# Expert weights in pages of 4 MB instead of 2 MB, and a 512-column output projection, in a two-block network on one core

## The chip, the core and the metric

The kernel runs on one core of a Trainium2 chip; the other cores are idle. The metric is the device time of one execution in microseconds (us), and the median of several executions is compared.

## What is computed

One token sequence of 256 tokens with 1024 features passes two blocks, all in float32. The first block mixes tokens (latent attention and banded attention of three dilations, gated and summed into `mix`), projects `mix` with `w_out`, adds the result to `x`, and then applies a mixture of 16 experts in which each expert chooses its tokens:

```
aff = softmax(h2 @ w_router); gate, idx = top_k(aff^T, 32)      # 32 tokens for each of 16 experts
xe  = h2[idx]                                                   # [16, 32, 1024]
hid = silu(xe @ w_gate) * (xe @ w_up)                           # w_gate, w_up: [16, 1024, 2048]
y   = (hid @ w_down) * gate                                     # w_down: [16, 2048, 1024]
x   = x + gt2 * scatter_add(y, idx); x = rmsnorm(x, g_final)
```

The second block (a state-space mixer, a linear recurrence and two convolved feed-forward layers, 1024 to 8192 to 1024) follows. Its code is the same in both kernels, except that its page buffers lie elsewhere.

## The kernel before

**Stages.** Everything is issued from one program, and the order within each engine's queue is made by a scheduler that goes by program order and readiness. All loads are issued from SyncE's queue (SP). The stages are, in the profiled execution: attention up to about 430 us, the output projection with `w_out` to 463 us, routing to 481 us, the 16 experts to 1387 us, the second block to the end.

**Weights by pages.** `page`/`wpage` (L200 to L211) loads 1 MB of weights into a buffer of 8 KB a partition; five such buffers make the pool `pages`. `split` (L216) makes a rounded half `wh` on ScalarE (L231) and the rest `wl` on VectorE (L232), and `three` (L237 to L245) multiplies hi by hi, hi by lo and lo by hi, so that one float32 product is three matmuls of a faster type. The value projections `v` (loop at L860) take pages of 256 columns: for each page and each of two token tiles, 8 chunks of the contraction times three matmuls of 256 columns go into one half of a PSUM bank (`proj_N`, L603). The output projection (loop at L936) does the same with four pages of `w_out`; after each page the product is scaled by `gt1` and added to `x1` (L947, L950), squares are summed (L951), the new columns are turned (L955) and multiplied by the router's weights (L961). After the fourth page come `inv_rms` (L967), written as an iteration on VectorE, the router's logits `lg` (L970), softmax, the turned affinities (L1016), four rounds of top-8 on VectorE (L1026 to L1036), and the choice as a one-hot matrix `oh` (`places`, L1042), by which `gather` (L1055) picks the tokens of experts 0 and 1 with 16 matmuls in 8 chunks `k`. Only when all eight chunks are done does expert 0 begin. The other 14 experts' tokens are gathered in expert 1's time, in rounds of four experts (L1083 to L1086).

**The experts.** An expert has 24 MB of weights: 8 pages of `w_gu` (a gate half and an up half, 8 KB a partition each) and 4 pages of `w_dn`, 2 MB each, of which a partition reads 16 KB in one piece. `load_epage` (L840) puts page after page into a ring of ten places, 20 MB in all: `swap`, four of `pages3`, two times two buffers of `pages` (these pages come as two transfers of 1 MB, 8 KB a partition, L852; all others as one, L854), two of `pages2`, one of `pages4`. `swap` can be loaded early; `pages2` lies where `split`'s halves were, `pages3` and `pages4` where the attention stage's tiles were. A transfer into a place is issued when the place's last readers are done. For a `w_gu` page PE does 8 products of 512 columns, four side by side in 32-column tiles of the array (L1093); each product is two matmul instructions in the trace. Then come `hid` (L1096, L1097), its transposes, 32 products of 512 columns for the four `w_dn` pages (L1114), the scaling by `gt2` (L1117), and four products with the scatter matrix `sel` onto the accumulators `acc` (L1120), which also hold `x`.

**The end of the experts.** Behind the last expert page SP issues `cols2` (L1142), two rows of norm weights (L1132, 0.5 MB each, one row read for all partitions), and two pages for the second block. From `acc` the norms (L1180 to L1193) give `xf`, which is turned (L1151) and multiplied with the two lead pages (L1160), for token tile 0 and then for tile 1.

## Time and profile before

| | before |
|---|---|
| median of 3 executions | 2277.21 us (2275.04 to 2279.51) |
| the profiled execution's own time | 2275.1 us |
| its span in the trace | 2273.3 us |
| TensorE busy (matmuls) | 1903.4 us, 84% of the span |
| VectorE, ScalarE, GpSimd busy | 44%, 35%, 11% |
| granted TensorE clock, mean | 0.92 of full speed |
| loads | 645.21 MB, of which the experts' weights are 402.65 MB |

The shares are averages over stages with different limits: in 40 slices of the span TensorE is busy over 90% in the first ten and in most of the last fifteen, and about 60% between them, where the sixteen DMA engines are busy all the time. So the stages are read one by one.

### The profile page before, as it was taken

What the parts mean: (1) busy time and instruction counts of PE and PEld (TensorE: products, weight loads), DVE (VectorE), ACT (ScalarE), POOL (GpSimd) and SP (SyncE); (2) the same over time, 40 slices, a digit from 0 to 9 for tenths busy, and PEclk for the clock granted to TensorE, in tenths of its full rate; (3) what the DMA queues carried; (4) which work ended last, traced back from release to release, by engine and by line L of the source; (5) the groups of instructions that cost most, each with busy time, mean ns of one, the idle gap of its engine ahead of it and who ended that gap; (6) DMA issues with size and microseconds to landing.
All of it is one profiled execution on the core that took longest, in us unless ns stands there. A gap on an engine that the chain in (4) does not pass through costs nothing.

```text
span 2273.3 us, 30086 instructions
## 1 busy us (share of the span) xinstructions
PE 1903.4 (84%) x12707; PEld 1317.6 (58%) x12707; DVE 1001.5 (44%) x1486; ACT 790.4 (35%) x1181; POOL 247.4 (11%) x176
## 2 busy tenths in 40 slices
PE   7999999988666666656656567999999999999998
PEld 5989999943111111111111115988888889888887
DVE  7867664331000000000000004867767777877775
ACT  2445454311000000000000004656666667666564
POOL 0100023100000000000000003110222222032222
PEclk9999999999767777887788879999999999999999
DMA  9357766679999999999999998543465646456552
GB/s 325 113 186 259 231 215 203 263 314 426 426 428 427 426 428 425 427 427 426 427 427 425 426 427 311 166 130 130 162 196 185 198 168 212 146 193 197 184 186 84
DMA packets 211166, 645.21 MB, mean 284 GB/s; under 512 B 8148, under 2 KB 162132, under 8 KB 178390
## 3 DMA queue, kind: packets, MB, share of 16 engines
q1 hardware_dynamic: 211032, 643.29, 74.5%
q8 instruction: 100, 1.64, 0.3%
q14 instruction: 34, 0.28, 0.0%
HBM read 641.95 MB, written 1.05 MB: 283 GB/s over the span
## 4 chain that ended last, share of the span: by engine, by line
PE 56%; DMA 38%; DVE 3%; ACT 2%; issue 1%; SPq 0%; DVEq 0%; ACTq 0%
DMA epage<-in_w_gu 25%; DMA epage<-in_w_dn 13%; PE up L1247 10%; PE up L1250 5%; PE ca L245 4%; PE ca L244 3%; PE ca L243 3%; PE lead L1160 2%; PE qk L243 2%; PE qk L245 2%; PE qk L244 2%; PE gu L1093 1%; PE v L245 1%; PE v L244 1%; PE v L243 1%; PE xbc L243 1%
## 5 line engine op out<-in xcount | busy, mean ns | idle before, releaser
L232 DVE TENSOR_TENSOR wl<-page,wh 128x2048 fp32r<-128x2048 f32 (+2 forms) x191 | 434.2, 2274 | 196.4 <-ACT wh L231 196.0
L1093 PE MATMUL gu<-epage,xeT 128*32 128x512 f32 x2048 | 318.9, 740 | 198.2 <-DMA epage<-in_w_gu 198.1
L231 ACT CAST wh<-page 128x2048 fp32r<-128x2048 f32 (+2 forms) x191 | 358.3, 1878 | 218.9 <-PE ca L245 64.8
L1247 PE MATMUL up<-hb,wh 128*128 128x512 f32 x960 | 331.9, 396 | 0.0
L1093 PEld LDWEIGHTS gu<-epage,xeT 128*32 128x32 f32 x2048 | 60.6, 122 | 435.6 <-DMA epage<-in_w_gu 327.7
L1096 ACT ACTIVATE hid<-gu 128x512 f32<-128x512 f32 x16 | 9.6, 598 | 785.1 <-PE gu L1093 785.1
L1114 PE MATMUL dn<-epage,hidT 128*32 128x512 f32 x1024 | 171.9, 803 | 99.3 <-DMA epage<-in_w_dn 90.5
L1250 PE MATMUL up<-hb,wl 128*128 128x256 f32 x960 | 248.0, 279 | 0.0
L1097 DVE TENSOR_TENSOR hid<-hid,gu 128x512 f32<-128x512 f32 x16 | 11.0, 689 | 491.3 <-PE gu L1093 491.3
L1247 PEld LDWEIGHTS up<-hb,wh 128*128 128x128 f32 x960 | 173.2, 188 | 33.6
L1250 PEld LDWEIGHTS up<-hb,wl 128*128 128x128 f32 x960 | 180.9, 188 | 10.6
L1114 PEld LDWEIGHTS dn<-epage,hidT 128*32 128x32 f32 x1024 | 32.2, 131 | 223.7 <-DMA epage<-in_w_dn 151.3
L1117 DVE TENSOR_TENSOR ye<-dn,gt 128x512 f32<-128x512 f32 x16 | 11.1, 692 | 286.0 <-PE dn L1114 286.0
L1280 DVE SCALAR_TENSOR_TENSOR cv<-ups,cols,cv 128x255 f32<-128x255 f32 x240 | 117.5, 502 | 28.1 <-ACT cv L1275 25.4
L243 PE MATMUL qk<-hh,wh 128*128 128x256 f32 x384 | 109.8, 286 | 0.0
L244 PE MATMUL qk<-hl,wh 128*128 128x256 f32 x384 | 109.0, 284 | 0.0
L245 PE MATMUL qk<-hh,wl 128*128 128x256 f32 x384 | 108.7, 283 | 0.0
L1308 POOL TENSOR_SCALAR lru_c<-cols 128x10 f32<-128x10 f32 x1 | 0.3, 251 | 954.1 <-PE dn L1114 954.1
L245 PE MATMUL ca<-wh,hdl 128*128 128x512 f32 x256 | 101.7, 397 | 0.0
L244 PE MATMUL ca<-wl,hdh 128*128 128x512 f32 x256 | 100.8, 394 | 0.0
L243 PE MATMUL ca<-wh,hdh 128*128 128x512 f32 x256 | 100.4, 392 | 0.0
L1275 ACT ACTIVATE cv<-ups,cols 128x256 f32<-128x256 f32 x120 | 71.1, 603 | 81.4 <-DVE ups L1255 81.2
(515 smaller groups left out, 3666.0 us busy)
## 6 DMA issues: line engine op xcount, KB each, us to landing
epage<-in_w_gu SPq DMA_DIRECT2D x102, 2048.0 KB, 29.8
epage<-in_w_dn SPq DMA_DIRECT2D x51, 2048.0 KB, 29.7
page<-in_ffn_w_up SPq DMA_DIRECT2D x64, 1024.0 KB, 5.5
epage<-in_w_gu SPq DMA_DIRECT2D x52, 1024.0 KB, 34.9
page<-in_w_in SPq DMA_DIRECT2D x46, 1024.0 KB, 5.4
page<-in_ffn_w_down SPq DMA_DIRECT2D x32, 1024.0 KB, 4.9
epage<-in_w_dn SPq DMA_DIRECT2D x26, 1024.0 KB, 34.3
page<-in_w_ada SPq DMA_DIRECT2D x24, 1024.0 KB, 6.5
```

Source lines behind the costliest of these rows:

```text
L231: act.copy(hi[p_], v[p_])
L232: (lo or dve).tensor_tensor(lw[p_], v[p_], hi[p_], ALU.subtract)
L243: pe.matmul(ps, lhsT=ah, rhs=bh, start=first and k == 0, stop=False)
L244: pe.matmul(ps, lhsT=ah, rhs=bl, start=False, stop=False)
L245: last_mm[0] = pe.matmul(ps, lhsT=al, rhs=bh, start=False, stop=last and k == n - 1)
L1093: pe.matmul(gu[i][32 * j:32 * j + 32, :], lhsT=xeT[:, k, 32 * e:32 * e + 32], rhs=pg[i][:, 512 * j:512 * j + 512], start=(k == 0), stop=(k ...
L1114: pe.matmul(pd[32 * q:32 * q + 32, :], lhsT=hT[:, 2 * c2 + cp, j, :], rhs=pg[c2][:, o:o + 512], start=(j == 0 and c2 == 0), stop=(j == 3 a ...
L1160: pe.matmul(pss[0][:, 256 * c + 128 * t:256 * c + 128 * t + 128], lhsT=pg[:, k, 128 * c:128 * c + 128], rhs=hf[:, k, nat(t)], start=(k == ...
L1247: wide = lambda: pe.matmul(ps, lhsT=wh[:, k, cc], rhs=hx[k][2], start=(k == 0), stop=(k == 7))
L1250: last_mm[0] = pe.matmul(ps[:, :256], lhsT=wl[:, k, cc], rhs=hx[k][0], start=False, stop=False)
L1275: act.activation(out=y[:, c], in_=ps[:, 256 * c:256 * c + 256], func=AF.Identity, scale=wcol(c, taps - 1), bias=bcol(c))
L1280: dve.scalar_tensor_tensor(y[:, c, o:], ps[:, 256 * c:256 * c + S - o], wcol(c, j), y[:, c, o:], ALU.mult, ALU.add)
```

## The change

- **Pages of 4 MB.** The host lays `w_gu` out so that two chunks `k` lie side by side, 32 KB a partition in one piece, 4 pages an expert, and `w_dn` so that a page holds two blocks of 256 output columns with all 16 chunks of the contraction, 2 pages an expert. `epage` uses a ring of five: four single places of 32 KB a partition and one made of `swap` and `place4`, whose page comes as two transfers of 2 MB. The first half of page 1 is loaded early, into `swap`. The last page of all comes as four transfers of 1 MB.
- **Places.** `swap` now lies below `pages`. The pool `pages` is closed before the experts and opened anew (`pagesb`) behind them. `place1` lies on the old `pages`, `place2` on `split`, `place3` to `place5` on the attention stage's tiles.
- **Down projection.** For each of four blocks of 256 columns, 16 products of 256 columns in four 32-column tiles, then the scaling and two scatter products of 256 columns. `gt2` holds 1024 columns, and `sel` and `sgate` lose their halves.
- **512 columns.** `v` and `w_out` pages hold 512 columns of half the contraction, so that a matmul has 512 columns and fills a bank. The attention loop has two steps of four heads. The first `w_out` page is multiplied ahead of the last four heads.
- **The end of the projection by token tiles.** Scaling, sum, squares, transposes and logits go by token tile (`wo_end`), the logits deferred (`flush`); the inverse norm is a square root on ScalarE and a reciprocal.
- **Routing.** The first top-8 round reads PSUM without a copy. Two of the eight chunks of experts 0 and 1 are gathered ahead of expert 0, the others between its chunks; `slots` comes behind its gate and up products. The other experts are gathered in seven rounds of two.
- **Norm rows.** They are loaded ahead of expert 12 into columns of `xeT` that are no longer read.

```diff
-    o["w_gu"] = gu.reshape(16, 8, 128, 4096)
-    o["w_dn"] = np.asarray(inp["w_down"])[0].reshape(16, 4, 4, 128, 1024).transpose(0, 1, 3, 2, 4).reshape(16, 4, 128, 4096)
+    o["w_gu"] = gu.reshape(16, 4, 2, 128, 4096).transpose(0, 1, 3, 2, 4).reshape(16, 4, 128, 8192)
+    o["w_dn"] = np.asarray(inp["w_down"])[0].reshape(16, 16, 128, 4, 256).transpose(0, 3, 2, 1, 4).reshape(16, 2, 2, 128, 4096).transpose(0, 1, 3, 2, 4).reshape(16, 2, 128, 8192)
...
-    pages = ctx.enter_context(tc.tile_pool(name="pages", bufs=1))
     sw = ctx.enter_context(ExitStack())
     swap = sw.enter_context(tc.tile_pool(name="swap", bufs=1))
+    pg_ = ctx.enter_context(ExitStack())
+    pages = pg_.enter_context(tc.tile_pool(name="pages", bufs=1))
...
-    ring = [(swap, "swap", 1)]
     expert_pages = []
     for e in range(NE):
-        expert_pages += [A["w_gu"][e, k] for k in range(8)] + [A["w_dn"][e, b] for b in range(4)]
...
-        pl, tag, nb = ring[cnt[0] % len(ring)]
+        expert_pages += [A["w_gu"][e, k] for k in range(4)] + [A["w_dn"][e, b] for b in range(2)]
+    cnt, ring, first_half = [0], [], []
+
+    def epart(t, src, o, n):
+        last_dma[0] = sync.dma_start(out=t, in_=src[:, o:o + n])
+        return [t[:, i:i + 2048] for i in range(0, t.shape[1], 2048)]
+
...
+    def epage():
+
+        pl = ring[cnt[0] % len(ring)]
         src = expert_pages[cnt[0]]
         cnt[0] += 1
...
-        if pl is pages:
-            v = [pl.tile([128, 2048], F32, name="epage", tag=tag, bufs=nb) for _ in range(2)]
-        else:
-            t = pl.tile([128, 4096], F32, name="epage", tag=tag, bufs=nb)
-            v = [t[:, :2048], t[:, 2048:]]
...
-        return ahead.pop(0) if ahead else load_epage()
...
-    for i in range(4):
-        if i == 3:
-            with tc.issue_after(last_dma[0].ins):
-                ahead.append(load_epage())
-            behind = last_dma[0]
+        if len(pl) == 2:
+            v = first_half.pop() if first_half else to_swap(src)
+            return v + epart(pl[1].tile([128, 4096], F32, name="epage", tag="half", bufs=1), src, 4096, 4096)
+        t = pl[0].tile([128, 8192], F32, name="epage", tag="place", bufs=1)
+        if cnt[0] < len(expert_pages):
+            return epart(t, src, 0, 8192)
+        return [epart(t[:, o:o + 2048], src, o, 2048)[0] for o in range(0, 8192, 2048)]
...
+    def proj_N2(w, c0, ps, tok):
+
+        for p_ in range(2):
+            wh, wl = split(wpage(w, c0, 512, 4 * p_, 4))
+            for t in range(2):
+                three(ps[t], [sl(k_, lambda a: a[:, tok(t)]) for k_ in h[4 * p_:4 * p_ + 4]],
+                      [(wh[:, k], wl[:, k]) for k in range(4)], p_ == 0, p_ == 1)
...
+    for ii in range(2):
...
-            pg = wpage(w_in, W_Q0 + 3072 * g + 2048 + 256 * i, 256)
-            ps = mm("v")
...
+            if ii == 1 and g == 2:
+                with tc.issue_after(last_dma[0].ins):
+                    first_half.append(to_swap(expert_pages[1]))
+            ps = [mm("v"), mm("v")]
+            proj_N2(w_in, W_Q0 + 3072 * g + 2048 + 512 * ii, ps, nat if g == 0 else par)
+            vt = dp.tile([128, 2, 512], F32, name=f"v{g}", tag=f"v{g}", bufs=1)
+            for t in range(2):
+                act.copy(vt[:, t], ps[t])
             v.append(vt)
...
-        pTs = []
-        for u in range(2):
-            hd = 2 * i + u
+        if ii == 1:
+
+            pso = [mm("wo"), mm("wo")]
+            w = wo_w(0, 0)
+            for t in range(2):
+                wo_mm(pso, w, 0, t)
...
+        pTs = [weights(0)]
+        for u in range(4):
+            if u < 3:
+                pTs.append(weights(u + 1))
...
-    for i in range(4):
-        pg = wpage(A["w_out"][0], 256 * i, 256)
-        wh, wl = split(pg)
-        ps = mm("wo")
-        for t in range(2):
-            three(ps[:, 256 * t:256 * t + 256], [sl(m_, lambda a: a[:, nat(t)]) for m_ in mx_],
-                  [(wh[:, k], wl[:, k]) for k in range(8)], True, True)
-        cs_ = slice(256 * i, 256 * i + 256)
...
-        dve.tensor_tensor(y, ps.rearrange("p (t n) -> p t n", t=2), gt1[:, None, cs_].to_broadcast([128, 2, 256]),
-                          ALU.mult)
-        for t in range(2):
-            dve.tensor_tensor(x1[:, t, cs_], x1[:, t, cs_], y[:, t], ALU.add)
-            sumsq(act, x1[:, t, cs_], y[:, t], x1q[t][:, i:i + 1])
...
+    def wo_end(g, t, ps):
...
+        for i in range(2):
+            o = 512 * g + 256 * i
+            cs_ = slice(o, o + 256)
+            y = rows3.tile([128, 256], F32, name="yo", tag="yo", bufs=3)
+            dve.tensor_tensor(y, ps[:, 256 * i:256 * i + 256], gt1[:, cs_], ALU.mult)
+            last = dve.tensor_tensor(x1[:, t, cs_], x1[:, t, cs_], y, ALU.add)
+            sumsq(act, x1[:, t, cs_], y, x1q[t][:, 2 * g + i:2 * g + i + 1])
             for c in range(2):
...
+        later.append(lambda: wo_logits(g, t, xT))
+        if g == 1:
...
+            dve.tensor_reduce(v, x1q[t], AX.X, ALU.add)
+            inv1[t] = inv_root(rows2, v, D)
+        return last
...
+    w = wo_w(0, 1)
+    for t in range(2):
+        wo_mm(pso, w, 1, t)
+        wo_end(0, t, pso[t])
+    pso = [mm("wo"), mm("wo")]
+    w = wo_w(2, 0)
+    for t in range(2):
+        wo_mm(pso, w, 0, t)
+    flush()
+    w = wo_w(2, 1)
+    for t in range(2):
+        wo_mm(pso, w, 1, t)
+        flush()
+        last = wo_end(1, t, pso[t])
+    flush()
...
-        dve.tensor_reduce(v[:, t:t + 1], x1q[t], AX.X, ALU.add)
-    inv1 = inv_rms(rows2, v, D)
...
-        dve.scalar_tensor_tensor(lg[:, t], pl_[t][:, :16], inv1[t], lsh, ALU.mult, ALU.add)
+        with tc.issue_after(last.ins):
+            dve.scalar_tensor_tensor(lg[:, t], pl_[t][:, :16], inv1[t], lsh, ALU.mult, ALU.add)
...
+    pg_.close()
...
-    pages2 = w2.enter_context(tc.tile_pool(name="pages2", bufs=2, reuse_waits="tile"))
-    pages3 = w2.enter_context(tc.tile_pool(name="pages3", bufs=4, reuse_waits="tile"))
-    pages4 = w2.enter_context(tc.tile_pool(name="pages4", bufs=1, reuse_waits="tile"))
-    ring = [(swap, "swap", 1)] + [(pages3, "page3", 4)] * 4 + [(pages, "page", NPAGE)] * 2 + \
-        [(pages2, "page2", 2)] * 2 + [(pages4, "page4", 1)]
+    place = [w2.enter_context(tc.tile_pool(name=f"place{i}", bufs=1, reuse_waits="tile")) for i in range(6)]
+    place[0].tile([128, 2048], F32, name="spare")
+    ring += [(place[5],), (swap, place[4]), (place[3],), (place[1],), (place[2],)]
...
+    residual([(0, 0)])
...
     with tc.issue_after(last.ins):
-        for t in range(2):
-            for n in range(2):
-                pe.matmul(acc[t][n], lhsT=ident, rhs=x1[:, t, 512 * n:512 * n + 512], start=True, stop=False)
+        residual([(0, 1), (1, 0), (1, 1)])
...
-    dve.tensor_copy(affT, pb_[:16, :256])
...
-        dve.max(out=g_, in_=affT)
-        dve.max_index(out=idx[:, 8 * r:8 * r + 8], in_max=g_, in_values=affT)
+        a_ = affT if r else pb_[:16, :256]
+        dve.max(out=g_, in_=a_)
+        dve.max_index(out=idx[:, 8 * r:8 * r + 8], in_max=g_, in_values=a_)
...
     act.copy(one16, K("one")[:16].to_broadcast([16, 128]))
-    oh = rp.tile([128, 2, 32 * 4], F32, name="oh")
+    oh = rp.tile([128, 2, 32 * 2], F32, name="oh")
...
-    gather(0, 64, rps)
...
+    def slots():
...
     for e in range(NE):
+        if e == 12:
+            for r, ap in zip(gg, (A["g_final"], A["norm_mix_pre_2"][0])):
+                sync.dma_start(out=r, in_=bass.AP(tensor=ap.tensor, offset=ap.offset, ap=[[0, 128], [256, 4], [1, 256]]))
         if e == 1:
-            for e0 in range(2, 16, 4):
-                places(e0, min(4, 16 - e0), cs)
-                gather(32 * e0, 32 * min(4, 16 - e0), cs)
+            for e0 in range(2, 16, 2):
+                places(e0, 2, cs)
+                gather(32 * e0, 64, cs)
             rt.close()
         gu = [cm(f"gu{i}") for i in range(2)]
+        if e == 0:
+            gather(0, 64, cs, [0, 1])
         for k in range(8):
-            pg = epage()
+            if k % 2 == 0:
+                pg4 = epage()
+            pg = pg4[2 * (k % 2):2 * (k % 2) + 2]
+            if e == 0 and 0 < k < 7:
+                gather(0, 64, cs, [k + 1])
             for i in range(2):
                 for j in range(4):
                     pe.matmul(gu[i][32 * j:32 * j + 32, :], lhsT=xeT[:, k, 32 * e:32 * e + 32],
                               rhs=pg[i][:, 512 * j:512 * j + 512], start=(k == 0), stop=(k == 7))
+        if e == 0:
+            slots()
...
-        sel = xp.tile([128, 2, S], F32, name="sel", tag="sel", bufs=1)
-        for n in range(2):
-            dve.tensor_scalar(sel[:, n], K("iota"), slot[:, e:e + 1], sgate[:, n, e:e + 1], ALU.is_equal, ALU.mult)
-        pd = cs("dn")
-        for j in range(4):
-            pg = epage()
-            for c2 in range(2):
-                for cp in range(2):
-                    for n in range(2):
-                        q = 2 * n + cp
-                        o = 1024 * cp + 512 * n
-                        pe.matmul(pd[32 * q:32 * q + 32, :], lhsT=hT[:, 2 * c2 + cp, j, :], rhs=pg[c2][:, o:o + 512],
-                                  start=(j == 0 and c2 == 0), stop=(j == 3 and c2 == 1))
-        ye = xp.tile([128, 512], F32, name="ye", tag="hid", bufs=1)
-        dve.tensor_tensor(ye, pd, gt2, ALU.mult)
-        for t in range(2):
-            for n in range(2):
-                pe.matmul(acc[t][n], lhsT=sel[:, n, nat(t)], rhs=ye,
-                          start=False, stop=(e == NE - 1))
+        sel = xp.tile([128, S], F32, name="sel", tag="sel", bufs=1)
+        dve.tensor_scalar(sel, K("iota"), slot[:, e:e + 1], sgate[:, e:e + 1], ALU.is_equal, ALU.mult)
+
+        for b in range(4):
+            if b % 2 == 0:
+                pg4 = epage()
+                pd = cs("dn")
+            pg = pg4[2 * (b % 2):2 * (b % 2) + 2]
+            bs = slice(256 * (b % 2), 256 * (b % 2) + 256)
+            for k in range(16):
+                q = k % 4
+                pe.matmul(pd[32 * q:32 * q + 32, bs], lhsT=hT[:, k % 4, k // 4, :],
+                          rhs=pg[k // 8][:, 256 * (k % 8):256 * (k % 8) + 256], start=(k < 4), stop=(k >= 12))
+            if b % 2 == 0:
+                ye_ = xp.tile([128, 512], F32, name="ye", tag="hid", bufs=1)
+            ye = ye_[:, bs]
+            dve.tensor_tensor(ye, pd[:, bs], gt2[:, 256 * b:256 * b + 256], ALU.mult)
+            for t in range(2):
+                pe.matmul(acc[t][b // 2][:, bs], lhsT=sel[:, nat(t)], rhs=ye, start=False, stop=(e == NE - 1 and b % 2 == 1))

...
+    pages = ctx.enter_context(tc.tile_pool(name="pagesb", bufs=1, reuse_waits="tile"))
...
-    gg = [row(A["g_final"]), row(A["norm_mix_pre_2"][0], "rowa")]
...
-        xf = xeT.rearrange("p k s -> p (k s)")[:, D * t:D * t + D]
+        xf = xeT[:, 4 * t:4 * t + 4, 256:512]
...
-            sumsq(act, acc[t][n], x1[:, t, hs[n]], v[n])
-            last = dve.tensor_tensor(xg[:, hs[n]], acc[t][n], gg[0][:, hs[n]], ALU.mult)
-        for n in range(2):
+            with tc.issue_after(last_root[0].ins) if t and n else ExitStack():
+                sumsq(act, acc[t][n], x1[:, t, hs[n]], v[n])
+            with tc.issue_after(last.ins) if t and n else ExitStack():
+                last_ = dve.tensor_tensor(four(xg[:, hs[n]]), four(acc[t][n]), gg[0][:, 2 * n:2 * n + 2], ALU.mult)
             sumsq(act, xg[:, hs[n]], x1[:, t, hs[n]], v[2 + n])
+        last = last_
```

## Rows read from the trace of the kernel before

**Rows 1.** The page's chain that ended last: share by engine, then by line.
```profile
PE 56%; DMA 38%; DVE 3%; ACT 2%; issue 1%; SPq 0%; DVEq 0%; ACTq 0%
DMA epage<-in_w_gu 25%; DMA epage<-in_w_dn 13%; PE up L1247 10%; PE up L1250 5%; PE ca L245 4%; PE ca L244 3%; PE ca L243 3%; PE lead L1160 2%; PE qk L243 2%; PE qk L245 2%; PE qk L244 2%; PE gu L1093 1%; PE v L245 1%; PE v L244 1%; PE v L243 1%; PE xbc L243 1%
```
**Rows 2.** Windows: stretch, length, engines' busy us (instructions), granted clock, DMA share, GB/s.
```profile
400.00:450.00 50.00, 49.82 (x402) 47.24 (x401) 19.01 (x21) 19.50 (x30) 7.70 (x8) 1.00 0.67 256
...
482.00:484.00 2.00, 2.00 (x24) 0.57 (x20) 0.37 (x2) 0.63 (x1) 0.00 (x0) 1.00 0.06 16
484.00:486.00 2.00, 2.00 (x24) 0.65 (x20) 0.00 (x0) 0.00 (x0) 0.00 (x0) 1.00 1.02 246
...
600.00:1300.00 700.00, 431.00 (x2412) 93.78 (x2412) 24.71 (x47) 13.03 (x22) 0.00 (x0) 0.79 1.01 426
...
1385.30:1395.00 9.70, 6.01 (x24) 2.43 (x24) 5.06 (x10) 5.77 (x19) 2.87 (x9) 1.00 1.01 325
```
**Rows 3.** Timeline of PE, expert 1 to 2: start, length, instruction, idle before.
```profile
565.64 1.06 PE L1093 MATMUL gu<-epage,xeT 128*32 128x512 f32 x8 [0.73 <-DMA epage<-in_w_gu]
...
570.61 1.94 PE L1093 MATMUL gu<-epage,xeT 128*32 128x512 f32 x8 [1.41 <-DMA epage<-in_w_gu]
...
595.08 1.92 PE L1093 MATMUL gu<-epage,xeT 128*32 128x512 f32 x16 [1.55 <-DMA epage<-in_w_gu]
```
**Rows 4.** Timeline of PE: 24 steps of 256 columns, 21 steps of 512 columns.
```profile
372.07 0.28 PE L243 MATMUL v<-wh,hh 128*128 128x256 f32 x1
...
374.95 0.28 PE L243 MATMUL v<-wh,hh 128*128 128x256 f32 x1
...
1720.32 0.39 PE L243 MATMUL ca<-wh,hdh 128*128 128x512 f32 x1
...
1725.22 0.39 PE L243 MATMUL ca<-wh,hdh 128*128 128x512 f32 x1
```
**Rows 5.** Timelines of DVE (four rows) and PE (two), projection's end to expert 0.
```profile
462.69 0.69 DVE L947 TENSOR_TENSOR yo<-wo,gt 128x512 f32<-128x512 f32 x1 [6.09 <-PE wo L245]
...
467.31 0.38 DVE L970 SCALAR_TENSOR_TENSOR lg<-logit,ir,lsh 128x16 f32<-128x16 f32 x2
...
470.04 0.41 DVE L1026 COPY affT<-affT 16x256 f32<-16x256 f32 x1 [0.77 <-PE affT L1016]
...
478.25 0.79 DVE L1065 TENSOR_SCALAR xeT<-xe,s2c 128x64 f32<-128x64 f32 x2 [0.89 <-PE xe L1060]
...
477.13 3.76 PE L1060 MATMUL xe<-oh,x 128*128 128x64 f32 x32 [0.47 <-DVE oh L1050]
...
481.04 13.94 PE L1093 MATMUL gu<-epage,xeT 128*32 128x512 f32 x128
```
**Rows 6.** Timeline of SP: issues of expert pages.
```profile
462.98 22.09 SPq L854 DMA_DIRECT2D epage<-in_w_dn  x4
```
**Rows 7.** Timeline of PE in expert 1: first and last gathers, then what follows.
```profile
508.62 1.05 PE L1060 MATMUL xe<-oh,x 128*128 128x128 f32 x8
...
534.53 2.26 PE L1060 MATMUL xe<-oh,x 128*128 128x64 f32 x16
...
540.75 6.21 PE L1093 MATMUL gu<-epage,xeT 128*32 128x512 f32 x56
...
549.23 5.36 PE L1114 MATMUL dn<-epage,hidT 128*32 128x512 f32 x48 [0.73 <-ACT hidT L1102]
```
**Rows 8.** Timeline at the end of the experts: PE, DVE, ACT, SP.
```profile
1360.37 0.33 SPq L1132 DMA_DIRECT2D row<-in_g_final  x1
...
1385.34 1.07 PE L1114 MATMUL dn<-epage,hidT 128*32 128x512 f32 x8 [1.42 <-DMA epage<-in_w_dn]
1386.47 0.69 DVE L1117 TENSOR_TENSOR ye<-dn,gt 128x512 f32<-128x512 f32 x1 [16.53 <-PE dn L1114]
...
1388.38 0.60 ACT L276 ACTIVATE x<-ca 128x512 f32<-128x512 f32 x1 [0.89 <-PE ca L1120]
...
1393.71 1.30 PE L1151 MATMUL tT<-kc,xeT 128*128 128x128 f32 x8 [2.80 <-DVE xeT L1192]
```

124 lines of the change are left out of this document (65 added, 59 removed).

## The prediction

> **What bounds the kernel now.** I read the chain that ended last first: matmuls hold 56% of it and waits for expert pages 38% [rows 1]. That says two regimes, so I went by windows. From 600 to 1300 us the DMA engines are busy all the time at 426 GB/s while PE is busy 431 of 700 us, at a mean granted clock of 0.79 (it moves between the two levels, 1.2 and 2.4 GHz) [rows 2]: there only the bytes and their rate count. Before the experts, and after them, PE is the bound, and a microsecond saved on PE's path is a microsecond.
>
> Between the regimes lies a gap that decides what the front is worth. The issue of pages 8 to 11 is held until about 485 us [rows 6], since the ring of 20 MB is full and nothing has been consumed; the DMA engines stand at a share of 0.06 in 482 to 484 us and are back in 484 to 486 [rows 2]. Expert 0 starts at 481.04 and spends 13.94 us on 128 instructions, 0.109 us each [rows 5]; page 0 takes 16 of them, 1.74 us, and is free at 482.8. The engines move again some 1.8 us later, at 484.6. From there on the stream runs to the last landing at 1385.34 [rows 8] without a pause. So the time is: when the first place comes free, plus the remaining bytes at the stream's rate, plus the tail from the last landing to the second block, plus the second block, which is left as it is.
>
> **Term 1, the first release.** (a) Wider matmuls. 24 steps of 256 columns take 2.88 us, 0.120 each, and 21 steps of 512 take 4.90, 0.233 each [rows 4]. `v` has 12 pages of 48 matmuls and `w_out` 4 of 48: 768 times 0.120 is 92.2 us; 384 times 0.233 is 89.6. PE is full through this stretch (49.82 of 50 us from 400 to 450 [rows 2]), so 2.6 us go. Their casts and splits keep their number (16 pages of 1 MB) and lie beside PE; without that cover each page would show up to some 4 us. Four heads of attention now stand uncovered by `v` instead of two, but a half of the projection is put ahead of them; I cost that at nothing. (b) The end by token tiles. From the first scaling to the logits is 462.69 to 467.31, 4.6 us [rows 5]. Afterwards VectorE has four half-size pieces (1.5 us), then a square (0.6), the reduction, root and reciprocal (0.8), while transposes, copies and logits run beside: about 4.1, so 0.5 us go. A bound is nothing to 2 us. (c) The copy ahead of top-8, 0.41 us [rows 5], lies on the path and goes, 0.4 us. (d) The gather of experts 0 and 1 begins at 477.13 and takes 3.76 us on PE for eight chunks, the first eviction on VectorE begins at 478.25, and expert 0 starts at 481.04 [rows 5]. With two chunks ahead it can start when the first is evicted, about 478.7: 2.3 us go. Sum: 5.8 us, expert 0 at 475.2.
>
> Against this, the first release is of a page twice as large, with a chunk's gather in it. Bare 64-column gathers ran four chunks in 2.26 us [rows 7], 0.57 each. So 2 times 1.74 plus 0.57 plus some 0.2 for the change of array tiles, 4.3 us: free at 479.5 instead of 482.8, **3.3 us earlier**. This needs a full ring by then. Page 4 goes into the old `split`, free after the last projection matmul at about 460; with 1.8 us and 9.7 us, or queued behind page 3, it lands by 472 to 475. It holds. Bounds: nothing (the front stalls where I see it full) to 6 us.
>
> **Term 2, the rate.** Landings are read from PE, which waits for each [rows 3]. From 565.64 to 570.61 a page of 2 MB came in two transfers of 8 KB a partition: 4.97 us. From 570.61 to 595.08 five pages came as one transfer each, 16 KB a partition: 4.894 each. A straight line through both gives 0.076 us a transfer and 4.818 us for 2 MB. A ring of ten is 8 times 4.894 and 2 times 4.97, 49.09 us for 20.97 MB, 427 GB/s, as the window has it. A page of 4 MB in one transfer would be 9.712, in two 9.788; a ring of five 48.64. Behind the first ring lie 91 of 96 pages, 18.2 rings at 0.45: **8.2 us less**. The trace has no 32 KB piece; the ends are nothing (a longer piece brings no more) and 16.6 (no fixed part left). A loss I leave out, since the longer of the two shown sizes is the faster. I take the line, as its two points are one doubling away.
>
> The Trainium skill speaks against this term: "DMA: Bandwidth & Descriptors", section on measured bandwidth, has 425 GB/s for one transfer as large as 16 MB, which is what this stream has already. By that row the term would be nothing. The same page puts the ceiling at 435 GB/s; the line's 4.818 us is 435.
>
> **Term 3, the norm rows.** Two loads of 0.5 MB are issued from 1360.37 on [rows 8], behind the last expert page, so that no expert waits for them. Afterwards they stand before expert 12, in the stream: 1.05 MB at 325 GB/s, the rate where such small loads run at full share [rows 2], is **3.2 us more**; at 426 GB/s 2.5. What they vacate, the DMA time behind the last page, lay beside the tail.
>
> **Term 4, the tail.** From the last landing, 1385.34, to the first transpose, 1393.71, are 8.4 us [rows 8]. Afterwards three of four column blocks are done when the last quarter page lands. Left are 16 instructions of 256 columns (1 to 1.9 us), scaling of half the width (0.45), the scatter (0.6), then for the last half the scaling by the norm weights beside the squares (0.8), its squares (0.8), root and reciprocal (0.6), the first half of `xf` (0.75) and hops of 0.1: some 5.9. **2.5 us less**. Bounds: 0 to 4. The lead pages have 1 MB less ahead of them and land some 5.5 us behind the last page; they stay hidden behind the norms, and would show from 8 us on.
>
> **What I cost at nothing.** The down projection's columns are as many as before, but in twice the instructions. In expert 1 a pair of instructions of 512 columns takes 0.11; for 256 columns the trace has no price: half of it, 0.055, or 0.1175, what 64-column gathers with a full load of weights take (3.76 over 32 [rows 5]). Per expert 7 to 15 us for 128 of them; the scatter halves. PE's slack in the stream (269 of 700 us, 22 us an expert) hides both. The low end is nearer, since its products have the same weights of 32 columns and the same four array tiles; I take 0.065. At the end of the stream 0.1175 would cost: the four quarters would queue, up to 5 us.
> The other experts' gathers are 56 chunks instead of 32. They run ahead of the ring's need: page m must be free by 479.5 + 9.73 m. The gathers took from 508.62 to 540.75 with gate and up products filling their waits [rows 7]. I expect expert 1 to start at about 508, its first page (page 6) to be done by 518 to 525 against 537.8, its fourth by 558 against 567. It fits, not by much.
>
> **The sum.** 3.3 + 8.2 - 3.2 + 2.5 = 10.8 us less. On the profiled execution's own 2275.1 us (span 2273.3 and 1.8 around it) that is 2264.3; it stands 2.1 below the median of the runs shown, 2277.2, so in their terms 2266.
>
> **Rivals.** *The rate stays at 427 GB/s.* For it: the step from 8 to 16 KB was only 1.5%, and the share of the DMA engines is already full. Against: the step is there. Then 2.6 us less, 2274.6; it decides if mid-stream shows 427. (It is the skill's 425 GB/s row, above; by that row the trace's 426 is already the end.)
> *Front or tail give nothing* (the attention stage stalls on single-buffered `v` tiles, or the quarters queue on PE): 3.3 or 2.5 us are lost, with 5 more if both turn to a loss: 2269 to 2274.
> *The coarse ring runs dry in expert 1.* If the scheduler puts the seven gather rounds ahead of expert 1's first page, page 6 is free after 508 + 56 times 0.57 + 4 for the placings + 3.7 = 548 at the soonest, 10 us late, and at a pace of 1.0 a chunk, which the mixed stretch had (32.1 us for 32 [rows 7]), 64 - 32 = 34 us late. Each us late is one of idle DMA. With 20 it is 9 us slower, 2286. It decides from 549 us on: there the gain is used up. Against it: in the trace the gate products filled the gathers' waits from the second chunk on.
>
> **How the numbers follow.** A measurement of this kernel can tell about 0.2% from no change, 4.6 us: below 2272.7 is faster, above 2281.8 slower. The forecast's own case, 2259 to 2272, has 0.60; the unchanged rate 0.15; front or tail lost 0.14, half of it still below 2272.7; the dry ring 0.11, nearly all slower. So faster 0.68, same 0.22, slower 0.10. The likeliest is 2266. The range has to take in the larger rate gain on one side and the unchanged rate on the other, and leaves out the dry ring: 2257 to 2277.
>
> **What would show it.** Right: in mid-stream landings 9.7 us apart and 430 or 431 GB/s where 426 stood; expert 0 at about 475; engines back at about 481; the last landing near 1376; first transpose 6 us behind it. Wrong: 427 GB/s in mid-stream (term 2), a share under 1 between 520 and 600 with SP waiting on PE (dry ring), PE idle between 390 and 455 (term 1), or products of the last three quarters back to back behind the last landing (term 4).

## The result, and the profile after

The changed kernel takes **2293.8 us** (median of 4 runs, 2292.1 to 2295.8) where the one before takes 2276.1 (2274.8 to 2279.5, 4 runs): a ratio of 1.0072, 95% interval 1.006 to 1.0084, **17.7 us slower**. The forecast was 2266, 10.8 us less than before. The profiled execution has a span of 2292.0 us against 2273.3, 18.7 us more.

In the chain that ended last, PE now has 64% where it had 56, and DMA 30% where it had 38 [rows 1]: PE's share of the chain has grown. The windows say where. Columns as in [rows 2]; of after, 110 us from the first release on, then mid-stream:

```profile
490.00:600.00 110.00, 101.92 (x747) 61.04 (x739) 19.20 (x60) 13.67 (x32) 0.00 (x0) 0.81 0.90 380
600.00:1300.00 700.00, 433.29 (x3336) 153.93 (x3326) 33.60 (x72) 14.19 (x24) 0.00 (x0) 0.80 1.00 430
```

In mid-stream the bytes come at 430 GB/s, as term 2 forecast, where they came at 426 [rows 2]. But ahead of that the DMA engines are busy only 90% of the time. The same view of after in stretches of 5 us:

```profile
530.00:535.00 5.00, 5.00 (x25) 5.00 (x25) 1.03 (x3) 1.21 (x3) 0.00 (x0) 0.50 1.00 433
...
555.00:560.00 5.00, 5.00 (x24) 2.46 (x23) 0.75 (x4) 0.40 (x1) 0.00 (x0) 0.50 0.45 187
560.00:565.00 5.00, 5.00 (x37) 3.83 (x31) 1.42 (x6) 1.21 (x3) 0.00 (x0) 0.98 0.64 223
...
570.00:575.00 5.00, 5.00 (x24) 2.94 (x27) 0.69 (x2) 0.81 (x2) 0.00 (x0) 0.50 0.37 157
575.00:580.00 5.00, 5.00 (x40) 1.31 (x36) 0.00 (x0) 0.00 (x0) 0.00 (x0) 0.77 0.39 108
580.00:585.00 5.00, 3.38 (x40) 1.33 (x36) 0.69 (x1) 1.18 (x2) 0.00 (x0) 1.00 0.78 334
```

What the shares lack to 1 from 545 to 585 us adds up to 12 us. Meanwhile PE is busy 37.9 of the 40 us, at a mean granted clock of 0.68; where the row says 0.50 it has the lower of its two levels throughout. The ring has run dry: SP's next issue waits for PE. Timeline of SP, issues of expert pages, and timeline of PE in expert 1, which answers to [rows 7]:

```profile
442.40 20.32 SPq L841 DMA_DIRECT2D epage<-in_w_gu  x4
462.81 24.63 SPq L841 DMA_DIRECT2D epage<-in_w_dn  x2
488.82 16.60 SPq L841 DMA_DIRECT2D epage<-in_w_gu  x5
511.96 14.45 SPq L841 DMA_DIRECT2D epage<-in_w_dn  x3
560.95 29.10 SPq L841 DMA_DIRECT2D epage<-in_w_gu  x4
```
```profile
525.96 2.26 PE L1109 MATMUL xe<-oh,x 128*128 128x64 f32 x16
...
528.91 6.52 PE L1109 MATMUL xe<-oh,x 128*128 128x64 f32 x32 [0.47 <-DVE oh L1099]
...
536.25 7.06 PE L1109 MATMUL xe<-oh,x 128*128 128x64 f32 x32 [0.47 <-DVE oh L1099]
...
560.82 4.57 PE L1109 MATMUL xe<-oh,x 128*128 128x64 f32 x32
...
566.08 6.45 PE L1109 MATMUL xe<-oh,x 128*128 128x64 f32 x32 [0.47 <-DVE oh L1099]
572.46 9.45 PE L1156 MATMUL gu<-epage,xeT 128*32 128x512 f32 x64
```

Between 526.4 (511.96 and 14.45) and 560.95 SP issues nothing. PE does bare rounds of 32 gather instructions of 64 columns, with no other products between them. Those at 528.91, 536.25 and 566.08 take 6.5 to 7.1 us each, the one at 560.82, with the clock at 0.98, takes 4.57; before the change 32 such took 3.76 [rows 5]. Expert 1's second page (page 7) is consumed at 560.9; SP can issue the successor of its third (page 8) only at 578.54, and the fourth, the last of its `w_gu` pages, is consumed at 581.9.

The front, on PE and in windows (answers to [rows 2, 5]):

```profile
473.73 0.26 PE L1097 MATMUL idxb<-blk,one 16*128 16x64 f32 x1 [1.46 <-DVE affT L1122]
474.46 7.02 PE L1109 MATMUL xe<-oh,x 128*128 128x64 f32 x32 [0.47 <-DVE oh L1099]
...
481.73 15.60 PE L1156 MATMUL gu<-epage,xeT 128*32 128x512 f32 x128
```
```profile
435.00:440.00 5.00, 5.00 (x29) 4.57 (x29) 0.95 (x2) 2.12 (x4) 0.94 (x2) 0.73 0.02 3
...
475.00:480.00 5.00, 4.92 (x24) 4.73 (x23) 1.03 (x3) 0.99 (x3) 0.00 (x0) 0.50 0.97 416
480.00:485.00 5.00, 5.00 (x25) 2.37 (x29) 1.02 (x4) 1.90 (x3) 0.00 (x0) 0.50 0.98 419
```

The places for experts 0 and 1 are broadcast at 473.73, some 2.6 us sooner than before the change, but all eight chunks are gathered ahead of expert 0, at half clock, and it starts at 481.73 where it started at 481.04 [rows 5]. The DMA engines are busy until 485 us, still filling the first ring, because SP issues the first page of it at 442.40 only.

The end, on PE (answers to [rows 8]):

```profile
1388.03 5.24 PE L1179 MATMUL dn<-epage,hidT 128*32 128x256 f32 x42 [2.97 <-DMA epage<-in_w_dn]
...
1394.26 2.80 PE L1179 MATMUL dn<-epage,hidT 128*32 128x256 f32 x48
...
1400.28 1.93 PE L1179 MATMUL dn<-epage,hidT 128*32 128x256 f32 x32
...
1407.87 1.97 PE L1217 MATMUL tT<-kc,xeT 128*128 128x128 f32 x8 [3.98 <-DVE xeT L1263]
1409.66 7.47 PE L1228 MATMUL lead<-hf,page 128*128 128x128 f32 x48
```
The last of these in the kernel before:
```profile
1395.02 5.87 PE L1160 MATMUL lead<-hf,page 128*128 128x128 f32 x48
```

Page 94 lands at 1388.03, and from there PE works through 128 products and four scatters without waiting for the last page's quarters. The first transpose is at 1407.87, 14.2 us later than before; from it to the second block's first product (1424.42, before 1408.18) are 16.6 us where 14.5 were. The first lead products take 7.47 us in place of 5.87, at a clock of 0.64 from 1410 to 1415 us where the kernel before had 1.00 from 1395 to 1400. The second block takes 2.5 us more: its first lines, `z`, take 37.1 to 37.4 us each where they took 36.4 to 36.6, with the clock at 0.98 between 1500 and 1600 us. Among the kernels below, whose second block is the same, it takes 865.7 to 867.7 us (866.1 in e1_spread, 867.7 in e12_inter), with no relation to their edits that we can see; why it does is open. 14.2, 2.1 and 2.5 make the 18.7 but for rounding.

### The profile page after: what moved, and what is told of

It reads as the page before. It is cut to its first block, busy times and chain, and to the rows that moved or that the text cites. A ratio compares the mean times of both kernels' runs of the same rounds, so it can differ in the third digit from the quotient of the medians.

```text
span 2292.0 us, 31696 instructions
## 1 busy us (share of the span) xinstructions
PE 1936.7 (84%) x13574; PEld 1407.0 (61%) x13574; DVE 1016.4 (44%) x1531; ACT 798.4 (35%) x1203; POOL 244.8 (11%) x176
## 4 chain that ended last, share of the span: by engine, by line
PE 64%; DMA 30%; DVE 4%; ACT 2%; issue 1%; POOL 0%; SPq 0%; DVEq 0%; ACTq 0%; POOLq 0%
DMA epage<-in_w_dn 15%; DMA epage<-in_w_gu 14%; PE up L1318 10%; PE up L1321 5%; PE gu L1156 4%; PE ca L246 3%; PE ca L245 3%; PE ca L244 3%; PE dn L1179 3%; PE xe L1109 2%; PE qk L246 2%; PE qk L245 2%; PE qk L244 2%; PE lead L1228 2%; PE ca L1186 1%; PE xbc L244 1%
## 5 line engine op out<-in xcount | busy, mean ns | idle before, releaser
L1156 PE MATMUL gu<-epage,xeT 128*32 128x512 f32 x2048 | 328.5, 786 | 200.9 <-DMA epage<-in_w_gu 200.9
L1156 PEld LDWEIGHTS gu<-epage,xeT 128*32 128x32 f32 x2048 | 74.4, 137 | 431.3 <-DMA epage<-in_w_gu 249.5
L1179 PE MATMUL dn<-epage,hidT 128*32 128x256 f32 x2048 | 154.7, 448 | 64.3 <-DMA epage<-in_w_dn 60.7
L1184 DVE TENSOR_TENSOR ye<-dn,gt 128x256 f32<-128x256 f32 x64 | 27.2, 425 | 290.8 <-PE dn L1179 290.8
L1179 PEld LDWEIGHTS dn<-epage,hidT 128*32 128x32 f32 x2048 | 73.0, 126 | 132.5 <-issue 104.1
L288 POOL TENSOR_SCALAR iq<-ssq 128x1 f32<-128x1 f32 x16 | 6.9, 428 | 1097.3 <-ACT x L277 963.1
L1186 PE MATMUL ca<-ye,sel 128*128 128x256 f32 x256 | 79.3, 436 | 29.7 <-DVE ye L1184 29.7
```

Source lines behind the costliest of these rows:

```text
L1156: pe.matmul(gu[i][32 * j:32 * j + 32, :], lhsT=xeT[:, k, 32 * e:32 * e + 32], rhs=pg[i][:, 512 * j:512 * j + 512], start=(k == 0), stop=(k ...
L1179: pe.matmul(pd[32 * q:32 * q + 32, bs], lhsT=hT[:, k % 4, k // 4, :], rhs=pg[k // 8][:, 256 * (k % 8):256 * (k % 8) + 256], start=(k < 4), ...
L1186: pe.matmul(acc[t][b // 2][:, bs], lhsT=sel[:, nat(t)], rhs=ye, start=False, stop=(e == NE - 1 and b % 2 == 1))
```

## The experiments

Three questions were put: what made the ring run dry, what held the first release, and what became of each term that was forecast. All edits are to the changed kernel.

**e1_spread**, one gather round per expert:

```
-        if e == 1:
-            for e0 in range(2, 16, 2):
-                places(e0, 2, cs)
-                gather(32 * e0, 64, cs)
-            rt.close()
+        if 1 <= e <= 7:
+            places(2 * e, 2, cs)
+            gather(64 * e, 64, cs)
+        if e == 7:
+            rt.close()
```

> One round of two experts' gathers at the head of each of experts 1 to 7, in place of seven rounds at the head of expert 1; nothing else. Theory A (the seven rounds in one burst hold page 6 until the ring is dry): the DMA engines' share stays near 1 from 490 to 600 us, the 12 us that they stood idle between 545 and 585 us come back, and the time is 2281 to 2284 us. Rival B (the ring of five large places runs dry whenever PE is late, and the gathers are only where it shows): the idle time moves to experts 2 to 7 and at most 4 us are gained, 2290 to 2294. Rival C (the 12 us are a matter of PE's clock at 0.50 in that stretch, not of how many chunks stand in it): the share stays under 1 in the same stretch, 2288 or more.

Measured: 2280.5 us (median of 10 runs), ratio to before 1.0011 (1.0001 to 1.002). The window from 490 to 600 us has 427 GB/s at a share of 1.00 where after had 380 at 0.90. So 13 of the 17.7 us were the burst of seven rounds. B falls, since no idle time came up elsewhere. C is not settled by it, although the time that it gave, 2288 or more, was missed: with the burst gone there is no stretch left in which that clock could matter.

**e2_four**, rounds of four, four, four and two experts as before the change:

```
-            for e0 in range(2, 16, 2):
-                places(e0, 2, cs)
-                gather(32 * e0, 64, cs)
+            for e0 in range(2, 16, 4):
+                places(e0, min(4, 16 - e0), cs)
+                gather(32 * e0, 32 * min(4, 16 - e0), cs)
```

(`blk` has four experts' columns, and `oh` lies in the unused place of 8 KB.)

> The gathers in expert 1 in rounds of four, four, four and two experts as in the kernel before (32 chunks in place of 56, up to 128 columns each); all else as after. Theory A: the burst is 24 chunks shorter, 13 us at full clock and more at the low one, so that page 6 is free by about 545 us and page 7 soon behind it; 8 to 12 of the 12 us come back, 2282 to 2286 us. Rival B (large places): the ring still dries by more than 8 us, 2290 or more. If the clock stays up with the wider gathers, as it did before the change, the two explanations (number of chunks, clock) go together; if it falls and the time still comes back, the number alone did it.

Measured: 2280.6 us (10 runs), ratio 1.0009 (0.9999 to 1.0018). The burst remains, with five large places, and the ring does not dry. The clock stayed at 1.00 from 490 to 565 us. Number and clock went together here too, so one more run was made.

**e13_wide7**, seven rounds as in after, the first six of four experts each (most experts are gathered twice, with the same values; `blk` and `oh` as in e2_four):

```
-                places(e0, 2, cs)
-                gather(32 * e0, 64, cs)
+                places(e0, min(4, 16 - e0), cs)
+                gather(32 * e0, 32 * min(4, 16 - e0), cs)
```

> All seven rounds stay in expert 1 as in after (56 chunks), but the first six gather four experts each, up to 128 columns wide, so that most experts are gathered twice with the same values; columns alone are added, 64 to 128 a product. Count theory (56 chunks in one burst are too many at any clock): the ring dries as in after or worse, 2291 us or more. Clock theory (64-column gathers, on which PE spends itself on loading weights, are what let the granted clock fall to 0.50, and at full clock 56 chunks would have fitted, as the prediction said): the clock stays at 1.00 between 525 and 560 us as in e2_four, at most 4 of the 12 us of idle DMA are left, 2282 to 2286 us.

Measured: 2280.4 us (10 runs), ratio 1.0012 (1.0003 to 1.0022): **13 us less than after, with more arithmetic**. Windows and PE's timeline of this kernel:

```profile
530.00:535.00 5.00, 4.42 (x27) 3.36 (x27) 2.02 (x6) 1.49 (x4) 0.00 (x0) 1.00 0.97 415
...
555.00:560.00 5.00, 4.53 (x36) 2.48 (x32) 1.28 (x4) 0.91 (x2) 0.00 (x0) 1.00 1.07 459
560.00:565.00 5.00, 4.87 (x35) 4.29 (x36) 1.39 (x5) 1.21 (x3) 0.00 (x0) 0.92 0.97 419
565.00:570.00 5.00, 4.88 (x33) 1.08 (x32) 0.00 (x0) 1.00 (x2) 0.00 (x0) 0.74 1.02 436
```
```profile
528.43 5.09 PE L1109 MATMUL xe<-spare,x 128*128 128x128 f32 x32 [0.54 <-DVE spare L1099]
...
544.63 5.09 PE L1109 MATMUL xe<-spare,x 128*128 128x128 f32 x32 [0.54 <-DVE spare L1099]
...
559.98 5.08 PE L1109 MATMUL xe<-spare,x 128*128 128x64 f32 x32 [0.47 <-DVE spare L1099]
564.98 4.90 PE L1156 MATMUL gu<-epage,xeT 128*32 128x512 f32 x32
```

The same 56 chunks, 48 of them with products twice as wide, are through by 565 us instead of 572.5, with expert 1's second page consumed at 543.9 (after: 560.9) and its fourth at 569.9 (581.9). A bare round takes 5.1 us instead of 6.5 to 7.1, at a clock of 1.00, and the engines' share stays near 1. The count theory falls; it was the clock.

The scheduler also set another order here: page 7's products begin behind the third round, in after behind the fourth. That is not the reason. At the prices that rows at full clock show (a bare round of 64 columns 3.76, a placing 0.8, eight gathers with eight products 2.0, a product instruction 0.109), after's own order would have page 7 done at about 547 us and page 8 at about 559, by an estimate. Counted from after's first held issue at 487.4, at 9.73 us a page, they were due at 555.5 and 565.3.

Why the clock falls is not shown. It falls in bare rounds of 64 columns: in after between 529 and 530 us, behind half a bare round, a wait of 0.47 us and the start of the next one; in e13 in the only such round of its burst, the seventh, at 559.98 (0.92 from 560 to 565, then 0.74). But the gather ahead of expert 0 in the kernel before, also such a round, had the full clock (3.76 us [rows 5]). And weight loads (PEld, the second engine) that fill the stretch are not the reason by themselves. In after they take 5.00 of 5.00 us from 530 to 535, at 0.50; in e13 3.36, at 1.00; in the kernel before, with the 256-column products of `w_out`, again 5.00, and there the clock is 1.00:

```profile
435.00:440.00 5.00, 5.00 (x44) 5.00 (x44) 0.00 (x0) 0.10 (x1) 0.00 (x0) 1.00 1.01 426
```

**e3_parts**, each page that has one place in two transfers of 2 MB:

```
-            return epart(t, src, 0, 8192)
+            return epart(t[:, :4096], src, 0, 4096) + epart(t[:, 4096:], src, 4096, 4096)
```

> Each of the pages with one place of its own is loaded in two transfers of 2 MB (16 KB of a partition) into the same place; waits and order of use as after. By the line of term 2 (0.076 us a transfer): 73 more transfers, 5.5 us more, mid-stream 427 GB/s, 2299 us. Rival (the 430 GB/s of after come from somewhere else than the longer pieces, as fewer waits at the ring): mid-stream stays at 430 GB/s, 2293 to 2295.

Measured: 2298.0 us (8 runs, 2282.6 to 2304.8, a wide scatter), ratio 1.0077 (1.0046 to 1.0109). The time alone is too scattered, as the ring dries in this kernel by varying amounts. The rate in mid-stream decides:

```profile
600.00:1300.00 700.00, 432.95 (x3320) 139.63 (x3312) 33.59 (x72) 14.19 (x24) 0.00 (x0) 0.82 1.01 427
```

With 16 KB of a partition in a piece 427 GB/s, with 32 KB 430, and nothing else changed: term 2's line holds. The edit doubles the number of transfers along with halving the piece; the two are not told apart.

**e4_norm_end** and **e8_spread_norm**: the two loads of norm rows moved from ahead of expert 12 to behind the loop over experts (the `for` with its `sync.dma_start(...)` stands behind that loop, without `if e == 12:`), in after and in e1_spread.

> The two loads of norm rows are issued behind the last expert page again, not ahead of expert 12. By term 3 the last page lands 2.5 to 3.2 us sooner; the rows land about 3 us behind it, well before the last products and squares are done, so the time is 2290.5 to 2291.5. Rival: the rows and the two lead pages behind them come late for the norm and for the first products of the second block, and the gain is given back, 2293 to 2296.

> e1_spread with the norm rows loaded behind the last expert page, as in the kernel before. Here no dry ring stands in the way of reading term 3: the last page lands 2.5 to 3.2 us sooner than in e1_spread, and the time is 2277 to 2278 us; if the rows are late for the norm, 2279 to 2281.

Measured: e4 2290.7 us (4 runs, ratio 1.0055, 1.0037 to 1.0073), but its profiled execution has a drier ring than after (364 GB/s from 490 to 600), so it tells nothing by itself. e8 2277.9 us (10 runs, ratio 1.0006, 0.9997 to 1.0016), 2.6 less than e1_spread. By the ratios, each to the runs of before beside it, the gain is about 1 us, and the two intervals overlap. The profiled executions show more: page 94 lands at 1373.88 us where it landed at 1377.80 in e1_spread, 3.9 sooner, of which 0.2 stem from a sooner restart. So term 3 has the sign and about the size that was forecast, 2.5 to 3.2; its tenths are not settled.

**e5_early, e6_resid, e7_both**: what held the first release, that is, the restart of the loads. The edits, on top of e1_spread, both in e7 (the first, of e5, also puts the products of `gps`, the scaling of `wr` and the logits' shift behind that `tick`, ahead of the heads of the second half; the copies into `gt1` stay where they were):

```
+    rows0 = rw0.enter_context(tc.tile_pool(name="rows0", bufs=1, side="right"))
+    wrs = rows0.tile([128, 8, 16], F32, name="wrs")
...
+            tick(len(todo))
+            gps = [mm("gt"), psA.tile([128, 512], F32, name="gta", tag="ada", bufs=1)]
...
         def weights(u):
```
```
-    residual([(0, 0)])
     aff = rp.tile([128, 2, 16], F32, name="aff")
...
-        residual([(0, 1), (1, 0), (1, 1)])
+        residual([(0, 0), (0, 1), (1, 0), (1, 1)])
```

> On top of e1_spread: the last reads of the attention stage's memory (the gate row's products, the router weights' scaling and the shift of the logits) are put ahead of the second half's heads, so that the first place comes free sooner. Theory F (restart is bound twice at about 488 us: the first ring is full at 488.0 and page 0 is consumed at 488): SP issues page 0 some 8 us sooner (434 us in place of 443.45), the ring is full by about 480, but page 0 is consumed at 488 still, since the gathers and the first products run at a clock of 0.50; the restart comes at 487 to 489 and the span is within 2 us of e1_spread's 2278.8. Rival G (the fill alone was the bound): restart at 481 to 484 and 2272 to 2275.

> On top of e1_spread: all four products of the residual stand behind the transposes of the affinities again, beside the top-8, as in the kernel before (one of the four was ahead of them). Theory F: PE works through the top-8 as it did before the change, the granted clock is back at full when the gather starts, the gather takes 3.8 us in place of 6.6 and expert 0 starts at 479 to 480; but the ring is full only at 488.0, so the restart stays at 488 and the span within 2 us of 2278.8. Rival H (the consumption alone was the bound): restart at 483 to 485, span 2273 to 2275. Rival I (the clock fell for another reason): gather over 5 us still, no change.

> e1_spread with both edits, of e5_early and of e6_resid. Theory F: only with both does the first release move: the ring is full by 480, page 0 (32 instructions of expert 0 at 0.109 us) is consumed at 483, the restart comes at 483 to 485, 4 to 6 us sooner than in e1_spread, and the time is 2275 to 2277 us. If F is wrong in its first half (fill), the restart stays at 488 and the time at 2280.

Measured: e5 2279.0 us and e6 2280.5 (one run each), e7 2278.1 (10 runs, 2270.1 to 2281.8, ratio 1.0001, 0.999 to 1.0013). Timeline of SP and a window of e5:

```profile
434.35 25.78 SPq L841 DMA_DIRECT2D epage<-in_w_gu  x4
460.22 25.37 SPq L841 DMA_DIRECT2D epage<-in_w_dn  x2
```
```profile
480.00:485.00 5.00, 5.00 (x32) 1.23 (x28) 0.00 (x1) 0.68 (x1) 0.00 (x0) 0.60 0.06 26
```

The times of e5 and e6, one run each, decide nothing; the traces do. In e5, with the first page issued 8 to 9 us sooner, the ring is full by about 480, and then the engines stand: page 0 is consumed at a clock of 0.60 and its successor issued at 485.6. There consumption binds. In e6 the gather takes 5.0 us, less than in e1_spread (6.6) but not the 3.8 that were expected, and expert 0's products still run at 0.50 from 480 to 485. The issue comes at 486.7, and until then the engines are busy: there the fill binds. In e7 gather and products run at full clock (expert 0 in 13.94 us), but its front was 4 us later in the profiled execution, with SP's first issue at 440.00. Its restart is at 486.3, 2.2 us sooner than in e1_spread where 4 to 6 were expected, and the time is 2.5 less. So two things bind at nearly the same moment, as theory F has it; its size was not reached by these two edits.

**e9_tail**, on top of e8: the last two pages in quarters; **e10_ring**, on top of e7 with the norm rows behind: page 0 is the one in two halves; **e11_all**: both; **e12_inter**: e11 with an order forced on expert 0's gathers.

```
-        if cnt[0] < len(expert_pages):
+        if cnt[0] < len(expert_pages) - 1:
```
```
-                    first_half.append(to_swap(expert_pages[1]))
+                    first_half.append(to_swap(expert_pages[0]))
...
-    ring += [(place[5],), (swap, place[4]), (place[3],), (place[1],), (place[2],)]
+    ring += [(swap, place[4]), (place[5],), (place[3],), (place[1],), (place[2],)]
```
```
-                gather(0, 64, cs, [k + 1])
+                with tc.issue_after(last_gu.ins):
+                    gather(0, 64, cs, [k + 1])
```

(In e10 to e12 the last page, now in two tiles, is still loaded in quarters. `last_gu` in e12 is expert 0's latest gate or up product.)

> On top of e8_spread_norm: the last two pages, not the last alone, come in quarters of 1 MB, so that the last expert's down products of the first half can start 7 us sooner and are out of the way when the last quarter lands. Theory T (term 4 failed because PE, not the landing, paces the last page: 96 products and three scatters queue behind page 94, which arrives whole): products of the last quarter start when it lands, from the last landing to the first transpose 6.5 to 7.5 us in place of 9.1, and the time is 2 to 2.5 us less, 2275.5 to 2276. Rival (the 9.1 us are the norm's own chain and the low clock): no more than 1 us.

> e7_both with the norm rows behind the last page, and the ring turned so that page 0, not page 1, is the one whose two halves lie in separate memory and come free one by one. Theory F: the first release is of 2 MB, after 16 instructions of expert 0, 1.7 us sooner at full clock, so the restart comes 1 to 2 us sooner than in e7_both where the ring is full by then; with 2.6 us for the norm rows the time is 2273.5 to 2275. If the fill is what binds in these runs, no sooner restart, 2275.5.

> e10_ring and e9_tail's edit together: the sum of both, 2271.5 to 2273.

> e11_all with the gather of chunks 2 to 7 for expert 0 held behind the products of the chunk before, which is the order that the prediction's term 1 (d) counted on and the scheduler did not give. If (d) was sound, expert 0's first products start 2 to 3 us sooner and the first 2 MB are free sooner by as much; the restart moves by 0 to 2 us, as far as the ring is full by then: 2270 to 2273. Rival: each chunk's eviction stands in PE's way and expert 0 takes some 4 us longer, with no gain, 2272 to 2275.

Measured: e9 2275.3 us (10 runs, ratio 0.9989, 0.9979 to 0.9999), 2.6 less than e8, which ran on another chip (by the ratios 3.9). e10 2272.4 (10 runs, 0.998, 0.997 to 0.999). e11 **2269.9** (7 runs, ratio **0.9968**, 0.9957 to 0.998): faster than both kernels, than the one before by 0.3%. e12 2269.9 (7 runs, 0.9971, 0.996 to 0.9983), no different from e11, so holding back chunks 3 to 7 is worth nothing once the first half page is consumed early. PE's timelines of e11, at the front and at the end:

```profile
471.74 1.10 PE L1114 MATMUL xe<-oh,x 128*128 128x64 f32 x8 [0.47 <-DVE oh L1104]
473.13 1.92 PE L1158 MATMUL gu<-epage,xeT 128*32 128x512 f32 x16 [0.29 <-DVE xeT L1119]
...
1376.20 1.07 PE L1181 MATMUL dn<-epage,hidT 128*32 128x256 f32 x16 [0.60 <-DMA epage<-in_w_dn]
1377.82 1.13 PE L1188 MATMUL ca<-ye,sel 128*128 128x256 f32 x4 [0.55 <-DVE ye L1186]
1383.48 1.97 PE L1221 MATMUL tT<-kc,xeT 128*128 128x128 f32 x8 [4.53 <-DVE xeT L1267]
```

With two halves the scheduler put only two chunks ahead, expert 0 starts at 473.13, and the engines' share stays at 0.96 and over through 480 to 490 us. The last quarter is waited for again (1376.20), and from there to the first transpose are 7.3 us. Theory T expected 6.5 to 7.5.

## Why the prediction was wrong, by its steps

**The step that failed most** is the one under "what I cost at nothing": "I expect expert 1 ... its first page (page 6) to be done by 518 to 525 ..., its fourth by 558 against 567. It fits, not by much." The first page was done at about 526. The second, page 7, which the working gave no figure for, was done at 560.9, where its line asks for 479.5 + 9.73 times 7, 547.6; the third, page 8, let its successor be issued at 578.5, where the line asks for 557.3; the fourth was done at 581.9. Even counted from the actual first held issue, 487.4, pages 7 and 8 were 5 and 13 us late, about as much as the 12 us of idle DMA. What failed is the price of a gather. It came from rows at full clock (a chunk in 0.57 bare, or 1.0 mixed [rows 7]). 64-column rounds, one after the other, had 0.50 of the clock, and bare rounds took 6.5 to 7.1 us for eight chunks in place of 3.76 [rows 5]. e13 shows that this was the point and the number of chunks was not: at full clock it did fit. It was as tight as was said: against the forecast line from 479.5 e13's third and fourth page (559.3 and 569.9) would have been 2 to 3 us late, but its own restart came at 486.8.

The outcome, not the mechanism, was among the rivals: the dry ring, held at 0.11 and priced at 2286 for 20 us of lateness. It cost 13 us (e1 and e13 against after). That rival had page 6 late, for the number of chunks and the order, at the clock of before; page 6 was in time, and pages 7 and 8 were late for the clock. (Its 34 us are right as 508 + 56 + 4 + 3.7 - 537.8, not as the 64 - 32 that is written.)

**Term 1, forecast -3.3.** (a) to (c), 3.5 us: the places came 2.6 sooner in after. Of this (a) gave 1.1 in place of 2.6 (the last scaling begins at 461.56 where it began at 462.69 [rows 5]); the clock was at 0.73 and 0.58 in the two stretches between 435 and 445 us, where the kernel before had 1.00. (b) gave 0.9 in place of 0.5: 3.7 us from there to the logits; the 4.1 that was written is not the sum of its terms, 2.9. In e11 the gather starts at 471.74, 5.4 us sooner than in [rows 5], with e5's edit in it; but in e7, with the same front, it starts at 477.27. The 0.2 for the change of array tiles had no row behind it; in e11 16 products and a chunk's gather take 2.44 us (473.13 to 475.57) where 1.74 and 0.57 make 2.31. The terms (a) to (c) were not tested one by one, and the front moves by several us from kernel to kernel. (d) failed: the scheduler put all eight chunks ahead, and at half clock 7.02 us stood where 3.76 had. And "This needs a full ring by then ... It holds" failed: only page 4's place was looked at, not page 0's, which the router weights and the gate row held until 442.40 (e5, which moves these, has the first issue at 434.35). So the ring was full at about 488 (in e1 the engines' share falls to 0.08 between 488 and 489). The first held page is issued at 487.4 (462.81 and 24.63) where it was at 485.1 [rows 6], 2.4 us later instead of 3.3 sooner.

**Term 2, forecast -8.2: right.** 381.7 MB (91 pages) at 426 and at 430 GB/s differ by 8.3 us, and e3 took the rate back to 427. The Trainium skill's page "DMA: Bandwidth & Descriptors", section on measured bandwidth, has 425 GB/s for one transfer of 16 MB, issued from GpSimd; here loads of 4 MB issued from SyncE, one behind the other, make a stream of 430, so the measurement decides against that row as an end.

**Term 3, forecast +3.2: right in kind**, 2.6 by the medians of e8 and e1, 3.7 by the landing of page 94.

**Term 4, forecast -2.5: wrong.** Of the 14.2 us by which the first transpose is late, 2.4 (restart), 12 (dry ring), -8.3 (rate) and 2.6 (norm rows) explain 8.7; the other 5.5 lie at the end of the stream and are not split further. The last landing itself cannot be read from PE in after, which does not wait for it. "Afterwards three of four column blocks are done when the last quarter page lands" did not hold in the sense that counts, that only the last block is left for PE, because page 94 came whole and PE, partly at half clock (42 products in 5.24 us), had 128 products queued. It stood among the rivals ("the quarters queue on PE") and as the bound "the four quarters would queue, up to 5 us", but tied to a price of 0.1175 a product; the price was 0.060 (32 in 1.93), and they queued all the same. With page 94 in quarters (e9, e11) the tail is 7.3 us, not 5.9: the scatter took 1.13 where 0.6 stood, and from there to the transpose 4.5 where 3.05 stood.

**The sum**: the rate was right, and the gains of the projection came in part; the three failures (ring full late, clock in the gathers, queue at the end) are all cases of PE or a place being late where only the stream was watched. With edits against all three, e11 stands at 2269.9, 7.0 us less than the runs of before on the same chip (2276.9). It is not the forecast kernel put right: its norm rows are back behind the stream, and without term 3 the forecast's terms make 14.0 us, so half of that is reached.

## What to carry to other kernels

Price a burst of many narrow products at both levels of the clock: a burst of wider products that does more arithmetic can be through sooner. For a ring, work out for each of the first pages who holds its place, and for each page of a burst when it must be free, not for the first and the last alone; and split the first page to be consumed as well as the last ones to arrive. A gain at one of two bounds that meet at the same moment shows nothing until the other one is moved too.

## What the runs showed of the hardware that was not expected

PE can show as busy without a pause and have half its clock. In after, 530 to 535 us, it is busy 5.00 of 5.00 us with 64-column products and their weight loads and has 0.50; with 128 columns (e13) it has 1.00 in the same stretch, and 32 products take 5.1 us instead of 6.5 to 7.1. What in the narrow rounds brings the clock down is open; loads that fill the stretch do not do it alone, as 435 to 440 us of the kernel before shows. And 4 MB in one transfer with 32 KB of a partition in a piece still bring something over two transfers with 16 KB: 430 GB/s against 427 (e3).
